# The constants of a kernel's own list schedule: delay, occupancy, a shared port and the delay of a transfer

## The chip, the cores and the metric

The kernel runs on one core of one Trainium2 chip. The metric is the device time of one execution in microseconds (us), as the median of several runs. The engines are TensorE (PE, with its weight loads as PEld), VectorE (DVE), ScalarE (ACT), GpSimd (POOL) and SyncE (SP), which issues all the transfers of this kernel.

## The reference

The reference is a two-layer diffusion trunk over 1024 latent tokens and 256 context tokens, all of width 1024, in fp32. Cut to what matters:

```python
for l in range(DEPTH):                                   # DEPTH = 2
    sh1, sc1, g1, sh2, sc2, g2 = ada_params(c[:, None, :], ada_w[l], ada_b[l])
    h  = modulate(rms_norm(x,  norm1_g[l]), sh1, sc1)    # latent, 1024 tokens
    hc = modulate(rms_norm(cx, norm1_g[l]), csh1, csc1)  # context, 256 tokens
    p = h @ w_in[l]                                      # 1024 -> 2304 columns
    y_a = fourier_mix(p[..., 0:256])                     # 2-D FFT as matmuls
    y_b = neighbourhood_attention(q, k, v, k_ctx, v_ctx, na_rpb[l], rows)
    y_c = spatial_gating(...)                            # gelu, layer norm, 128x128 mixing
    o_d = diff_latent(...)                               # softmax(s1) - lam * softmax(s2), then @ v
    y = concatenate([y_a, y_b, y_c, diff_post(o_d)]) @ w_out[l]
    # layer 0 does the same for the context tokens
    x = x + g1 * y
    h2 = modulate(rms_norm(x, norm2_g[l]), sh2, sc2)
    x = x + g2 * sq_relu_mlp(h2, w_ff1[l], w_ff2[l])     # 1024 -> 4096 -> 1024
return rms_norm(x, final_g)
```

## The kernel before

Tokens lie in three blocks: two of 512 latent tokens (0 and 1) and one of 256 context tokens (2). Activations are held with channels on the partitions. Every fp32 product is made of three products of a shorter type, FP32R: an operand is split into a high and a low part (`hh`/`hl` for activations, `wh`/`wl` for weights), and `mm3` adds high by high, high by low and low by high into one bank of PSUM. The high part is a copy on ScalarE. The low part is a subtraction on GpSimd or VectorE. Weights that layer 1 needs, and part of those of layer 0's MLP, are split ahead of time and kept in DRAM as `wd`; they are loaded as `wh`/`wl` by plain transfers.

The stages follow one another in time, with some overlap: the start (root mean squares `nacc`, `nss`, `nr`, `nrb`; the modulation parameters `ada`, whose weighted sums `aa` run on VectorE and GpSimd; the first projections `pj`, `pv`), the mixers of layer 0, its MLP, the mixers of layer 1, its MLP (the products `sx`, `sy`), and the final norm. In an attention mixer, scores (`ds`, or `nsl` and `nsc`) come from TensorE. VectorE takes their maximum and ScalarE the exponential `e`. VectorE and GpSimd normalise `e`, TensorE transposes it (`tp`), ScalarE and VectorE evacuate the transpose as a high and a low part (`pt`, `npt`), and TensorE multiplies these by the values (`pvd`, `pvn`).

No instruction is issued where it is written. The program text records every operation in a `Plan`, with the operations on which it depends and a rank. `Plan.cost` gives each a time, and `Plan.flush` makes a list schedule over the five engines: it takes the engine that can start earliest, and on it, among the operations that are ready by the plan's own clock, the one of lowest rank. An operation counts as ready once all that it waits for has ended by that clock, plus `LAT` where the two are on different engines. All instructions are then emitted in this one order (all of them at L286), and each engine of the chip works its own instructions off in that order, waiting where a result is not there yet. So the plan's clock sets the order alone; it delays nothing by itself. In the plan, an instruction of SP takes 0.06 us to issue, a transfer holds the transfer clock for its bytes at 320 bytes per ns (at least 0.3 us), and its result is there a fixed time later.

Of the kernel before, what the change touches and what calls it, by code (L numbers as in the profile page):

```python
# [11 lines left out]
F32R = mybir.dt.float32r  # L12
# [4 lines left out]
PSUM = bass.MemoryType.PSUM  # L17
# [16 lines left out]
class Plan:  # L34
# [3 lines left out]

    LAT = 0.13

    def __init__(self, tc):
        self.tc, self.nc = tc, tc.nc
        self.rank = self.erank = 0.0
        self.ops = []
        self.done = 0
        self.hist = {}
        self.tiles = {}
        self.tags = {}  # L50
        self.masks = {}
        self.free = {}
        self.idle = []
        self.dma_free = 0.0


    def pool(self, pool):
# [102 lines left out]
    def cost(self, eng, method, outs, ins, kw):  # L160
        def width(a):
            n = 1
            for _, k in a.ap[1:]:
                n *= k
            return n

        n = max(width(a) for a in outs + ins)
        if eng == "tensor":
            n = width(outs[0])
            c = 1 if ins[0].dtype == F32R else 2 if method == "transpose" else 4  # L170
            return max(n, 128 if c == 4 else 64) * c / 2400.0
        if eng == "sync":
            b = 4
            for _, k in outs[0].ap:
                b *= k
            return b
        if eng == "scalar":
            return 0.093 + n / 1200.0 + (0.13 if kw.get("accum_out") is not None else 0.0)
        if eng == "vector":
            ptr = any(isinstance(kw.get(k), bass.AP) for k in ("scalar", "scalar1", "scalar2"))  # L180
            fast = method in ("tensor_scalar", "tensor_copy", "memset") and all(a.space != PSUM for a in outs + ins)
            return 0.065 + 0.065 * ptr + n / (1920.0 if fast else 960.0)
        return 0.1 + n / 470.0


    def flush(self):
        ops, base = self.ops, self.done
        n = len(ops)
        left, succ, ready = {}, {}, {}
        tiles, tags = self.tiles, self.tags  # L190
        waiting = {}
        engines = ("tensor", "vector", "scalar", "gpsimd", "sync")
        future = {e: [] for e in engines}
        avail = {e: [] for e in engines}

        def allocate(key):
            q = tags[key]
            while q[2] < q[0] and q[1]:
                t = q[1].pop(0)
                q[2] += 1  # L200
                tiles[t][2] = q[3]
                for i in waiting.pop(t, ()):
                    settle(i, q[3])

        def settle(i, t):
            ready[i] = max(ready[i], t)
            left[i] -= 1
            if left[i] == 0:
                heapq.heappush(future[ops[i][0]], (ready[i], i))

        pend = {}
        for i in range(base, n):
            for t in ops[i][5]:
                pend[t] = pend.get(t, 0) + 1

        def release(t):
            q = tags[tiles[t][0]]
            if q[1]:
                q[2] -= 1
                q[3] = max(q[3], tiles[t][3])  # L220
                allocate(tiles[t][0])
            else:
                self.idle.append(t)

        idle, self.idle = self.idle, []
        for t in idle:
            if t not in pend:
                release(t)
        for key in tags:
            allocate(key)  # L230
        for i in range(base, n):
            o = ops[i]
            left[i] = 1
            ready[i] = 0.0
            for j in o[4]:
                if j >= base:
                    left[i] += 1
                    succ.setdefault(j, []).append(i)
                else:
                    ready[i] = max(ready[i], ops[j][8])  # L240
            for t in o[5]:
                if tiles[t][2] is None:
                    left[i] += 1
                    waiting.setdefault(t, []).append(i)
                else:
                    ready[i] = max(ready[i], tiles[t][2])
            settle(i, 0.0)
        order = []
        while len(order) < n - base:
            best = None  # L250
            for e in engines:
                f = self.free.get(e, 0.0)
                if avail[e]:
                    s = f
                elif future[e]:
                    s = max(f, future[e][0][0])
                else:
                    continue
                if best is None or s < best[0]:
                    best = (s, e)  # L260
            s, e = best
            while future[e] and future[e][0][0] <= s:
                _, i = heapq.heappop(future[e])
                heapq.heappush(avail[e], (ops[i][6], i))
            _, i = heapq.heappop(avail[e])
            o = ops[i]
            if e == "sync":
                self.free[e] = s + 0.06
                self.dma_free = max(self.dma_free, s) + max(0.3, o[7] / 320e3)
                end = self.dma_free + 1.9  # L270
            else:
                end = s + o[7]
                self.free[e] = end
            o[8] = end + self.LAT
            order.append(i)
            for k in succ.get(i, ()):
                settle(k, end if e == "tensor" and ops[k][0] == "tensor" else o[8])
            for t in o[5]:
                pend[t] -= 1
                tl = tiles[t]  # L280
                tl[3] = max(tl[3], o[8])
                if pend[t] == 0:
                    release(t)
        for i in order:
            o = ops[i]
            ins = o[1](*o[2], **o[3])  # L286
            self.tc.keep_in_program_order(ins)
            o[1] = o[2] = o[3] = None
        self.done = n
# [1861 lines left out]
```

## Time and profile before

| what | value |
|---|---|
| time, median of 3 runs (lowest to highest) | 3067.94 us (3063.21 to 3068.87) |
| the profiled execution: its time, its span | 3058.95 us, 3057.1 us |
| mean granted TensorE clock of the profiled execution | 0.972 |
| busy share of the span: PE, DVE, ACT, POOL | 93%, 66%, 45%, 24% |
| moved from and to HBM | 388.58 MB, 162.88 MB |

The profile is of one execution on the chip. Times in it are us from the start of the span. "Idle before" is the time for which an engine had nothing to do before an instruction, and the name behind it is what released that instruction. The granted clock is a share of TensorE's full 2.4 GHz; at the lower of its two levels, 1.2 GHz, the same product takes twice as long.

### The profile page before, as it was taken

How to read it: one execution, taken by the hardware profiler on the slowest of the kernel's cores; microseconds unless marked ns; L12 is line 12 of the kernel's file. 1: busy time of each engine (PE TensorE's matmuls, PEld its weight loads, DVE VectorE, ACT ScalarE, POOL GpSimd, SP SyncE). 2: the span in 40 equal slices, each digit the busy share in tenths (PEclk: the TensorE clock that was granted, in tenths of full speed). 3: DMA queues.
4: the chain of work that ended last, by engine and by line, in shares of the span. 5: the costliest groups of instructions: out<-in, count | busy, mean ns of one | idle time of the engine just before them, and what ended most of it. 6: DMA issues, size and time to landing. Idle time of an engine off the chain costs nothing. (4 is left out here: it accounts for less than half of the span.)

```text
span 3057.1 us, 42917 instructions
## 1 busy us (share of the span) xinstructions
PE 2854.0 (93%) x14994; PEld 2348.7 (77%) x14994; DVE 2028.2 (66%) x3721; ACT 1370.7 (45%) x2974; POOL 738.7 (24%) x507
## 2 busy tenths in 40 slices
PE   6798999999999999999999888998998999999997
PEld 3776787776788888888888777877786778878876
DVE  7577886695766676664433737786784875576765
ACT  5476565584423233222122426555573544454332
POOL 5235222343521121121111303311110022122200
PEclk8998999999999999999999999999999999999998
DMA  6644345777347886673111463455688664464465
GB/s 229 194 133 134 106 125 153 245 251 251 98 146 260 274 275 217 221 239 126 59 46 38 145 200 126 132 163 160 215 298 290 226 215 144 145 217 150 150 230 176
DMA packets 291632, 550.60 MB, mean 180 GB/s; under 512 B 35924, under 2 KB 84692, under 8 KB 288344
## 3 DMA queue, kind: packets, MB, share of 16 engines
q1 hardware_dynamic: 291416, 547.86, 54.6%
q8 instruction: 118, 1.93, 0.3%
q14 instruction: 98, 0.80, 0.1%
HBM read 388.58 MB, written 162.88 MB: 180 GB/s over the span
## 5 line engine op out<-in xcount | busy, mean ns | idle before, releaser
L286 POOL TENSOR_TENSOR wl<-wr,wh 128x512 fp32r<-128x512 f32 (+2 forms) x260 | 361.1, 1410 | 928.8 <-ACT wh L286 887.9
L286 PE MATMUL sx<-bq,sh 128*128 128x512 f32 x2304 | 548.5, 396 | 9.5 <-ACT q L286 3.4
L286 PEld LDWEIGHTS sx<-bq,sh 128*128 128x128 f32 x2304 | 430.5, 188 | 121.1 <-DVE bq L286 6.5
L286 DVE TENSOR_REDUCE mx<-ds 128x1 f32<-128x512 f32 (+1 forms) x320 | 218.5, 686 | 135.0 <-PE ds L286 133.1
L286 ACT ACTIVATE e<-ds,nm 128x512 f32<-128x512 f32 (+1 forms) x400 | 241.3, 611 | 122.8 <-DVE nm L286 112.9
L286 ACT ACTIVATE wh<-wr 128x512 fp32r<-128x512 f32 (+2 forms) x260 | 152.4, 614 | 315.5 <-issue 137.3
L286 PE MATMUL f<-hidh,wh 128*128 128x512 f32 (+1 forms) x768 | 276.8, 360 | 6.3 <-ACT hh L286 4.1
L286 PE MATMUL f<-hidl,wh 128*128 128x512 f32 (+1 forms) x768 | 275.8, 359 | 0.0
L286 PE MATMUL f<-hidh,wl 128*128 128x512 f32 (+1 forms) x768 | 275.6, 359 | 0.0
L286 PE MATMUL f<-hh,wh 128*128 128x512 f32 (+1 forms) x768 | 274.5, 357 | 0.0
L286 PE MATMUL f<-hl,wh 128*128 128x512 f32 (+1 forms) x768 | 274.2, 357 | 0.0
L286 PE MATMUL f<-hh,wl 128*128 128x512 f32 (+1 forms) x768 | 274.2, 357 | 0.0
L286 PE MATMUL pj<-hh,wh 128*128 128x512 f32 (+1 forms) x512 | 194.5, 380 | 24.0 <-DMA wh<-wd 11.5
L286 DVE SCALAR_TENSOR_TENSOR x<-f,ada,x 128x512 f32<-128x512 f32 (+1 forms) x192 | 125.6, 659 | 135.3 <-PE f L286 134.7
L286 PE MATMUL pj<-hl,wh 128*128 128x512 f32 (+1 forms) x512 | 193.9, 379 | 2.0 <-POOL hl L286 1.2
L286 PE MATMUL pj<-hh,wl 128*128 128x512 f32 (+1 forms) x512 | 192.7, 377 | 1.0 <-DMA wl<-wd 1.0
L286 ACT ACTIVATE sh<-wq 128x512 fp32r<-128x512 f32 x160 | 99.3, 628 | 203.4 <-DMA wd<-sh 47.9
L286 POOL TENSOR_TENSOR e<-e 128x1280 f32<-128x1280 f32 (+1 forms) x36 | 98.4, 2733 | 380.4 <-DVE e L286 226.1
L286 POOL TENSOR_TENSOR ws<-wq 128x512 f32<-128x512 f32 x54 | 77.7, 1439 | 421.5 <-DVE sh L286 205.6
L286 PE MATMUL ds<-dks,dqs 128*128 128x512 f32 (+1 forms) x400 | 144.1, 397 | 31.0 <-ACT e L286 17.7
L286 DVE TENSOR_TENSOR fr<-fr 128x512 f32<-128x512 f32 (+1 forms) x96 | 83.6, 870 | 132.7 <-ACT fr L286 132.4
L286 PEld LDWEIGHTS f<-hidh,wh 128*128 128x128 f32 x768 | 145.4, 189 | 30.4 <-ACT hh L286 4.5
(316 smaller groups left out, 6555.8 us busy)
## 6 DMA issues: line engine op xcount, KB each, us to landing
wd<-sh SPq DMA_DIRECT2D x99, 512.0 KB, 4.0
wr<-in_w_ff SPq DMA_DIRECT2D x144, 256.0 KB, 3.1
ar<-in_ada_w SPq DMA_DIRECT2D x112, 256.0 KB, 4.0
bq<-hid SPq DMA_DIRECT2D x24, 1024.0 KB, 6.5
wq<-in_w_ff1s SPq DMA_DIRECT2D x76, 256.0 KB, 2.9
sh<-wd SPq DMA_DIRECT2D x66, 256.0 KB, 4.4
wq<-in_w_ff2s SPq DMA_DIRECT2D x64, 256.0 KB, 3.8
wr<-in_ada_w SPq DMA_DIRECT2D x48, 256.0 KB, 3.9
```

The source lines that it names most:

```text
L286: ins = o[1](*o[2], **o[3])
```

## The change

The change edits the numbers and rules of `Plan` alone; what is computed and the set of instructions stay as they are.

- `LAT`, the delay between an operation's end and its use on another engine, is 0.22 us instead of 0.13.
- The occupancy of an FP32R product is max(0.112, 0.006 + n/2265) instead of max(n, 64)/2400 (for n = 512: 0.232 instead of 0.213; for 256: 0.119 instead of 0.107). Transposes and fp32 products stay within a few ns.
- On ScalarE the fixed part is 0.055 if an input lies in PSUM and 0.105 if not (0.093 before), and an accumulated sum adds 0.17 instead of 0.13. On GpSimd the time is 0.13 + n/457 instead of 0.1 + n/470 (for n = 512: 1.25 instead of 1.19). On VectorE a scalar operand from memory adds 0.06 instead of 0.065.
- A new rule, `shares`, names the operations that use a port common to VectorE and GpSimd: every operation of GpSimd, and those of VectorE that read nothing from PSUM and have two inputs or are a `tensor_scalar` or `tensor_copy`. In `flush` such an operation starts no earlier than the last one that shared the port has ended.
- The delay of a transfer after its bytes is 2.6 us instead of 1.9.

```diff
-    LAT = 0.13
+    LAT = 0.22
...
+        self.port = 0.0
...
             n = width(outs[0])
-            c = 1 if ins[0].dtype == F32R else 2 if method == "transpose" else 4
-            return max(n, 128 if c == 4 else 64) * c / 2400.0
+            if ins[0].dtype == F32R:
+                return max(0.112, 0.006 + n / 2265.0)
+            if method == "transpose":
+                return 0.107
+            return max(0.224, n / 600.0)
...
         if eng == "scalar":
-            return 0.093 + n / 1200.0 + (0.13 if kw.get("accum_out") is not None else 0.0)
+            near = any(a.space == PSUM for a in ins)
+            return (0.055 if near else 0.105) + n / 1200.0 + (0.17 if kw.get("accum_out") is not None else 0.0)
...
-            return 0.065 + 0.065 * ptr + n / (1920.0 if fast else 960.0)
-        return 0.1 + n / 470.0
+            return 0.065 + 0.06 * ptr + n / (1920.0 if fast else 960.0)
+        return 0.13 + n / 457.0
+
+    def shares(self, o):
+
+        if o[0] == "gpsimd":
+            return True
+        if o[0] != "vector":
+            return False
+        ins = [v for k, v in o[3].items() if k in ("in_", "in0", "in1") and isinstance(v, bass.AP)]
+        if any(a.space == PSUM for a in ins):
+            return False
+        return len(ins) > 1 or o[9] in ("tensor_scalar", "tensor_copy")
...
                 self.dma_free = max(self.dma_free, s) + max(0.3, o[7] / 320e3)
-                end = self.dma_free + 1.9
+                end = self.dma_free + 2.6
             else:
+                if self.shares(o):
+                    s = max(s, self.port)
+                    self.port = s + o[7]
                 end = s + o[7]
```

What this does to the order is seen in the instructions of each engine. The order of the two MLPs is nearly the same before and after; within the mixers most instructions move by a few places. Three places follow. In a row stand the line, the operation, the output and the inputs with their buffer numbers, and the shape; xN is N such in a row.

The first place is the start. On GpSimd, once the last `aa` is done, before:

```order
L286 TENSOR_TENSOR aa_124<-aa_124,adaw_116 128x512 x7
L286 TENSOR_TENSOR hl0_134<-x0_93,hh0_133 128x512
L286 TENSOR_TENSOR hl0_134<-x0_95,hh0_133 128x512
L286 TENSOR_TENSOR hl0_134<-x0_94,hh0_133 128x512
L286 TENSOR_TENSOR hl0_134<-x0_93,hh0_133 128x512
L286 TENSOR_TENSOR wvl_206<-wr_203,wvh_205 128x512
```

And on GpSimd after:

```order
L305 TENSOR_TENSOR aa_124<-aa_124,adaw_116 128x512 x7
L305 TENSOR_TENSOR wvl_206<-wr_203,wvh_205 128x512
L305 TENSOR_TENSOR wvl_206<-wr_204,wvh_205 128x512
L305 TENSOR_TENSOR wvl_210<-wr_207,wvh_209 128x512
L305 TENSOR_TENSOR wvl_210<-wr_208,wvh_209 128x512
L305 TENSOR_TENSOR hl0_134<-x0_93,hh0_133 128x512
L305 TENSOR_TENSOR hl0_134<-x0_94,hh0_133 128x512
```

The four low parts of the value weights (`wvl`) move ahead of the four low parts of block 0's activations (`hl0`), which the first projections read. On TensorE, the sums of squares of block 1 (`nss_143`) stand here before, behind 32 of the 48 products of the first two projections (`pj_185`, `pj_196`):

```order
L286 MATMUL pj_185<-hl0_134,wh_183 128x512
L286 MATMUL pj_185<-hh0_133,wl_184 128x512
L286 MATMUL pj_196<-hl0_134,wh_194 128x512
L286 MATMUL nss_143<-ones_79,nacc_135 128x1 x4
L286 MATMUL pj_196<-hh0_133,wl_195 128x512
L286 MATMUL pj_196<-hh0_133,wh_194 128x512
```

And after, the same sums stand here:

```order
L305 MATMUL ada_132<-ones_79,aa_124 128x1 x4
L305 MATMUL pj_185<-hh0_133,wh_183 128x512
L305 MATMUL pj_196<-hh0_133,wh_194 128x512
L305 MATMUL nss_143<-ones_79,nacc_135 128x1 x4
L305 MATMUL pj_185<-hl0_134,wh_183 128x512
L305 MATMUL pj_185<-hh0_133,wl_184 128x512
```

They move up to behind the first two of the 48 products.

The second place is in the differential attention of layer 1, on TensorE, where scores (`ds`) alternate with the gating mixer's `sgo` and a projection (`pj_3320`). Before:

```order
L286 MATMUL sgo_3317<-fs_3270 64x128
L286 MATMUL ds_3640<-dks_3550,dqs_3622 128x256
L286 MATMUL ds_3640<-dks_3551,dqs_3622 128x256
L286 MATMUL sgo_3317<-fs_3270 64x128 x3
L286 MATMUL ds_3642<-dks_3551,dqs_3622 128x512
L286 MATMUL pj_3320<-hh0_2975,wh_3318 128x512
L286 MATMUL pj_3320<-hl0_2976,wh_3318 128x512
```

And after, the last `sgo` and what follows them:

```order
L305 MATMUL ds_3640<-dks_3550,dqs_3622 128x256
L305 MATMUL ds_3640<-dks_3551,dqs_3622 128x256
L305 MATMUL sgo_3317<-fs_3270 64x128 x2
L305 MATMUL pj_3320<-hh0_2975,wh_3318 128x512
L305 MATMUL pj_3320<-hl0_2976,wh_3318 128x512
L305 MATMUL pj_3320<-hh0_2975,wl_3319 128x512
```

A little further on, after:

```order
L305 MATMUL pj_3320<-hh0_2975,wh_3318 128x512
L305 MATMUL pj_3320<-hl0_2976,wh_3318 128x512
L305 MATMUL ds_3642<-dks_3551,dqs_3622 128x512
L305 MATMUL pj_3320<-hh0_2975,wl_3319 128x512
L305 MATMUL pj_3320<-hh0_2975,wh_3318 128x512
L305 MATMUL pj_3320<-hl0_2976,wh_3318 128x512
L305 MATMUL ds_3643<-dks_3551,dqs_3622 128x512
```

Eleven products of `pj_3320` now stand ahead of `ds_3642`, where none stood before (some of them lie between the two pieces above).

The third place is in the neighbourhood attention of layer 1, on TensorE, beside the output projection `wo`. Before:

```order
L286 MATMUL tp_4246<-ident_78,e_4236 128x128 x4
L286 MATMUL wo_4320<-fs_4303,wh_4317 128x512
L286 MATMUL wo_4320<-yl4_4304,wh_4317 128x512
L286 MATMUL wo_4320<-fs_4303,wl_4318 128x512
L286 MATMUL wo_4324<-fs_4301,wh_4321 128x512
L286 MATMUL tp_4247<-ident_78,e_4236 128x128 x2
L286 MATMUL wo_4324<-fs_4302,wh_4321 128x512
L286 MATMUL pvn_4248<-npt_4243,nsb_4141 128x256
```

And after:

```order
L305 MATMUL tp_4246<-ident_78,e_4236 128x128 x4
L305 MATMUL tp_4247<-ident_78,e_4236 128x128 x2
L305 MATMUL pvn_4248<-npt_4243,nsb_4141 128x256
L305 MATMUL pvn_4248<-npt_4244,nsb_4141 128x256
L305 MATMUL wo_4339<-yh1_4325,wh_4340 128x512
```

The transposes `tp_4245`, `tp_4246` and `tp_4247` are evacuated into slices of `npt_4243` (high) and `npt_4244` (low), which the products `pvn_4248` read. The `wo` products that stood between the transposes and these products have moved to other places.

## Rows read from the trace of the kernel before

**Rows 1.** The page's first part: busy time of each engine, its share of the span, and its instructions.

```profile
PE 2854.0 (93%) x14994; PEld 2348.7 (77%) x14994; DVE 2028.2 (66%) x3721; ACT 1370.7 (45%) x2974; POOL 738.7 (24%) x507
```

**Rows 2.** Busy time of each engine (with its instructions), the granted TensorE clock, the share of the DMA engines and GB/s, in six stretches: start, mixers of layer 0, its MLP, mixers of layer 1, its MLP, final norm.

```profile
0.00:150.00 150.00, 103.97 (x527) 80.14 (x528) 92.36 (x169) 71.57 (x131) 56.06 (x44) 0.90 0.64 211
150.00:930.00 780.00, 727.94 (x4195) 588.89 (x4194) 569.88 (x1230) 429.36 (x1086) 269.99 (x194) 0.97 0.52 167
930.00:1720.00 790.00, 788.79 (x4089) 667.80 (x4088) 442.84 (x627) 212.95 (x386) 165.44 (x116) 1.00 0.52 172
1720.00:2475.00 755.00, 673.39 (x3793) 563.75 (x3792) 544.48 (x1168) 403.06 (x989) 140.59 (x77) 0.95 0.62 200
2475.00:2960.00 485.00, 484.27 (x2074) 387.97 (x2073) 318.00 (x430) 227.31 (x347) 99.22 (x70) 1.00 0.50 171
2960.00:3057.00 97.00, 75.62 (x326) 60.14 (x324) 60.68 (x102) 26.47 (x38) 7.43 (x6) 0.90 0.59 201
```

**Rows 3.** The waits of TensorE over the whole span: what waited for what, us in total, how often, the longest.

```profile
PE nss L286 <- DVE nacc L286: 23.6, 7, 14.9
PE ds L286 <- ACT e L286: 17.7, 24, 2.5
PE pj L286 <- DMA wh<-wd: 11.5, 2, 8.2
PE nrb L286 <- DVE nr L286: 11.4, 5, 4.3
...
PE drb L286 <- DVE drw L286: 6.0, 3, 3.0
...
PE fmid L286 <- DVE m L286: 4.8, 1, 4.8
PE tp L286 <- DVE e L286: 4.8, 6, 1.5
...
PE tp L286 <- DVE npt L286: 3.0, 5, 1.3
```

**Rows 4.** The timeline of TensorE at the start: start in us, us, engine, line, operation, out<-in, how many, and in brackets the idle time before it with its releaser.

```profile
65.28 0.40 PE L286 MATMUL pj<-hl,wh 128*128 128x512 f32 x1
69.47 1.05 PE L286 MATMUL nss<-ones,nacc 128*128 128x1 f32 x8 [3.80 <-DVE nacc L286]
...
71.10 0.63 PE L286 MATMUL pj<-hl,wh 128*128 128x512 f32 x1
71.53 0.63 PE L286 MATMUL pj<-hh,wl 128*128 128x512 f32 x1
...
94.90 0.77 PE L286 MATMUL pj<-hh,wh 128*128 128x512 f32 x1 [6.16 <-DVE nr L286]
```

**Rows 5.** The timelines of VectorE and GpSimd at the start, columns as in rows 4.

```profile
19.61 0.75 DVE L286 SCALAR_TENSOR_TENSOR aa<-adaw,sc,aa 128x512 f32<-128x512 f32 x1
...
36.65 8.34 DVE L286 SCALAR_TENSOR_TENSOR aa<-adaw,sc,aa 128x512 f32<-128x512 f32 x5
...
53.87 1.28 POOL L286 TENSOR_TENSOR hl<-x,hh 128x512 fp32r<-128x512 f32 x1 [6.41 <-ACT x L286]
...
62.29 6.58 POOL L286 TENSOR_TENSOR wvl<-wr,wvh 128x512 fp32r<-128x512 f32 x4 [1.14 <-ACT wvh L286]
```

**Rows 6.** The timelines of TensorE and ScalarE at the second place, columns as in rows 4.

```profile
1989.02 0.65 PE L286 MATMUL sgo<-fs 128*64 128x128 f32 x6
1991.95 0.50 PE L286 MATMUL ds<-dks,dqs 128*128 128x512 f32 x1 [2.28 <-ACT e L286]
...
1992.57 0.63 PE L286 MATMUL pj<-hl,wh 128*128 128x512 f32 x1
1993.00 0.63 PE L286 MATMUL pj<-hh,wl 128*128 128x512 f32 x1
...
1991.12 0.69 ACT L286 ACTIVATE e<-ds,nm 128x512 f32<-128x512 f32 x1
```

**Rows 7.** The timelines of TensorE, ScalarE and VectorE at the third place, columns as in rows 4.

```profile
2310.60 0.62 PE L286 MATMUL tp<-ident,e 128*128 128x128 f32 x4
...
2311.30 0.39 PE L286 MATMUL wo<-yl,wh 128*128 128x512 f32 x1
2311.53 0.40 PE L286 MATMUL wo<-fs,wl 128*128 128x512 f32 x1
...
2312.44 0.52 PE L286 MATMUL pvn<-npt,nsb 128*128 128x256 f32 x3
...
2311.37 0.60 ACT L286 ACTIVATE npt<-tp 128x512 fp32r<-128x512 f32 x1
...
2312.14 0.75 DVE L286 SCALAR_TENSOR_TENSOR xo<-wo,ada,xo 128x512 f32<-128x512 f32 x1
2312.81 0.68 DVE L286 TENSOR_TENSOR npt<-tp,npt 128x512 fp32r<-128x512 f32 x1
```

**Rows 8.** The transfers: a stretch of SP's queue, TensorE behind it (columns as in rows 4), and from the page's part on issues two groups with the KB of each and the median us from issue to landing.

```profile
2084.18 7.58 SPq L286 DMA_DIRECT2D nvw<-vt  x16
...
2097.96 0.79 PE L286 MATMUL pj<-hh,wh 128*128 128x512 f32 x1 [8.21 <-DMA wh<-wd]
...
wr<-in_w_ff SPq DMA_DIRECT2D x144, 256.0 KB, 3.1
...
sh<-wd SPq DMA_DIRECT2D x66, 256.0 KB, 4.4
```

## What the change was predicted to do

> **What bounds the kernel now.** I read the page's busy times first: TensorE is busy for 2854.0 us of a span of 3057.1, far ahead of VectorE with 2028.2 [rows 1]. So about 203 us of the span are left on TensorE, and a change of order can only win there. The table by stretch says where they lie [rows 2]: 46 us at the start (150 less 103.97), 52 in the mixers of layer 0, 1 in its MLP, 82 in the mixers of layer 1, 1 in its MLP, 21 in the final norm. The two MLPs keep TensorE busy at a granted clock of 1.00. Their order is all but unchanged, so I expect 0 from these 1275 us. What is at stake are the start and the mixers. The granted clock is 0.90, 0.97 and 0.95 there, so a gap costs a little more than its length.
>
> The waits name the causes [rows 3]. TensorE waits for the sums of squares (`nss`, 23.6, of which 14.9 once, at the very start, for the first data), for exponentials before it may write the next scores (`ds` behind `e`, 17.7 in 24 pieces), for loads of weights (`pj`, 11.5), for `nrb` 11.4, `drb` 6.0, `fmid` 4.8, and for transposes and their evacuation (`tp` 4.8 and 3.0). These are many short waits for chains on other engines. TensorE had work elsewhere in its queue, but the plan took the chain for shorter than it is and put the waiting instruction too early.
>
> **The change part by part.** It removes and adds no instruction. Each term is a sum of waits gone and waits come. To find the places I went through the two orders and added up TensorE's work between each waiting instruction and the one that starts its chain (0.23 us for a product of 512 columns, from 2311.30 to 2311.53 in [rows 7]). That work is the cover.
>
> *A, the start.* Before, `nss` waits 3.80 us behind 32 of the 48 first products, and later a product waits 6.16 [rows 4], since block 1's modulation comes late. After the first wait the products run 0.43 apart (71.10 to 71.53) instead of 0.23, the lower of the two clocks; for some eight products that is 1.6. Afterwards, block 1's sums stand 30 products further ahead and its chain begins earlier. I let both waits go, with the 1.6 and some 2 of small ones behind them: -13.6. Against it, GpSimd now makes four `wvl` before the first `hl0`. They took 6.58 [rows 5]. TensorE's third product reads that `hl0`, and all 46 left stand behind it: +6.6 if nothing hides it. The third product starts later, but from there on the products need not stop. The sum is -7, with the ends -13.6 (the `wvl` are hidden) and +6.6 (the whole `wvl`, no wait saved).
>
> *B, waits that get more cover.* The second place is the clearest. `ds` waits 2.28 for `e` [rows 6]; eleven products now lie ahead of it, 11 x 0.233 = 2.6, so the wait goes. What follows it at the lower clock (0.43 from 1992.57 to 1993.00) runs faster too. There are 33 places of this kind in the mixers. What they can give is limited by the waits of their kinds: `ds` 17.7, `nss` beyond the start 4.9 (23.6 - 14.9 - 3.8), `nrb` some 3 (11.4 less two long ones of about 4.2 at the start and the end), `drb` 6.0, `fmid` 4.8, `tp` 7.8, in all 44 [rows 3]. At some of them the order is as before, two of the three `drb` for example. I take somewhat over half, -25. The ends are -40 (nearly all) and -12 (a quarter).
>
> *C, waits that get less cover.* At 31 places less work than before lies between transposes and the products that read them. At the third place [rows 7] the four transposes end at about 2311.0, ScalarE's `npt` starts at 2311.37, and VectorE's runs from 2312.81 to 2313.49, some 2.4 us after the transposes; 0.75 of this is `xo`, which stands ahead of it on VectorE. After the change there are two transposes, one `wo` and a few `pvn` of about 0.12 in between, some 1.2. So 0.45 (without `xo`) to 1.2 is missing there. Behind the waiting `pvn` stands all of TensorE's queue. Over 31 places nothing is the lower end (the plan now counts the longer delay, so it moved them where its clock shows the evacuation as done), and 1.3 at each, 40, the upper. I take 0.55, near the lower value of this place, as half of the places lose less cover than this one: +17. I believe B more than C, because B's waits are measured and C's rest on queues that move as well.
>
> *D, the transfers.* Landing takes 3.1 to 4.4 us for 256 KB [rows 8]. The plan's old figure for this is 0.82 + 1.9 + 0.13 = 2.85, the new one 3.64, so by the rows the new one is nearer. It can only help loads that are issued in time. The longest wait for one, 8.21 us at 2097.96, comes from SP, which is busy with sixteen `nvw` stores for 7.58 us ahead of the load, 0.47 each; the plan counts 0.06 for each, before and after, and the place is the same in SP's queue. I take -2, with ends 0 and -6. Here a rule of the Trainium skill speaks against the edit: "DMA: Bandwidth & Descriptors", section "Anatomy of one DMA", puts a transfer's time at about 2.0 us plus its bytes at 436 GB/s, for another kind of issue than this kernel's. For 256 KB that is an estimate of 2.6 us, nearer to the old figure than to the new one; D would be 0 and the time 3051. The rows show longer times than this rule for every group here.
>
> *E, the clock.* Each gap of over 2 us is followed by products at 0.43 instead of 0.23 [rows 4, 6], about 1.4 us for seven. Three such gaps go in B, one or two may come in C: -2, with ends -4 and +2.
>
> The occupancies of ScalarE, GpSimd and VectorE and the port have no term of their own; they show in A to C through the order. The port's part is real: five `aa` took 8.34 on VectorE while GpSimd worked on its own, 1.67 each, one without that 0.75 [rows 5]. But the engines exclude each other before as after, and only the plan's knowledge of it is new.
>
> The sum: -7 - 25 + 17 - 2 - 2 = -19. The profiled execution took 3058.95 us, 9 less than the median of 3067.94 and less than the fastest of its three runs. I take the difference off the median: 3067.94 - 19 = **3049 us**.
>
> **The rivals.** A difference of 0.2%, 6.1 us, is about what a measurement of this kernel can tell from no change.
>
> 1. *The gain without its price.* C is 0 and B is 40: -7 - 40 - 2 - 3 = -52, 3016; with part of it 3014 to 3030. For it speaks that the new durations match the rows (0.232 against 0.23 apart for a product). Against it, 31 places with less cover are many for none to wait.
> 2. *The waits only move.* B and C cancel, and the start gives nothing: 3062 to 3074. For it: by counts of cover alone the two are nearly even, 33 places against 31, and VectorE, 66% busy, is a second queue in which every saved wait may meet another operation.
> 3. *Slower: the transposes.* C is the full 40 and B only 12: -7 - 12 + 40 - 3 = +18, 3086, and with the upper end of A 3100. The mechanism is the third place, 31 times over: `pvn` stands directly behind its transposes, while `npt` waits on VectorE behind work of other stages. With B at 12 it decides from C = 28 on (0.9 us a place), with B at 25 from 41 on.
> 4. *Slower at the start.* GpSimd's `wvl` hold it and the port for 6.58 us ahead of `hl0`, no wait of the start goes, and the mixers come out even: +6.6, less 0 to 4 of D and E, 3070 to 3076. The Trainium skill, "SBUF — State Buffer", section "Who interferes with whom", calls the port pair an exclusive lock which whoever comes first holds for the whole instruction; by that rule VectorE's own `hl0` would be held up beside the four `wvl` as well. The 1.67 against 0.75 above agrees.
>
> **How the numbers follow.** My forecast, 3030 to 3061, has 0.42; rival 1 0.15, rival 2 0.19, rival 3 0.14, rival 4 0.10 (0.04 of it within 0.2%). Faster is 0.42 + 0.15 = 0.57, the same 0.19 + 0.04 = 0.23, slower 0.14 + 0.06 = 0.20. The range for 8 in 10 is 3020 to 3080: it leaves out half of rival 1 (0.07) and most of rival 3 (0.13). The likeliest case's own range is 3030 to 3061.
>
> **What would show it.** For A: no wait of `nss` behind products at 65 us, in its place one of `pj` for `hl` of up to 6.6, and the wait of 6.16 gone. For B: `ds` behind `e` at 12 or less in total instead of 17.7, and no wait at the second place. For C: the waits of `tp`, `pvn` and `pvd` for `e`, `npt` and `pt` up by some 17 in sum. For D: the wait of 8.2 is still there. In the table by stretch, TensorE's idle time should fall from 46 to about 40 at the start and by some 12 in all over both mixers, with both MLPs at 1. I am wrong if the waits for `npt`, `pt` and `e` grow by over 35 us, if a transfer that was on time comes late behind SP's queue, or if idle time moves into the MLPs or the final norm, to which I gave nothing.

## The result and the profile after

The changed kernel took 3025.64 us (3020.74 to 3026.14) against 3067.78 us of the kernel before in the same comparison: a ratio of 0.9862, with a 95% interval of 0.9845 to 0.9879. That is 42 us less where 19 were forecast. The time lies in the stated range of 3020 to 3080, but the gain is over twice the forecast.

The profiled execution took 3025.96 us with a span of 3024.2, so here the trace agrees with the median. The trace of before was 9 us under its median. Between the two traces, 33 us are to be explained, and 9 of the 42 lie between that trace and the runs.

The page's first part of the changed kernel, columns as in [rows 1]:

```profile
PE 2854.4 (94%) x14994; PEld 2357.3 (78%) x14994; DVE 2005.3 (66%) x3721; ACT 1363.8 (45%) x2974; POOL 728.5 (24%) x507
```

TensorE is busy for the same 2854 us. VectorE and GpSimd are busy for 23 and 10 us less with the same instructions, so they hold each other up less here. That is no sign of the port's rule: kernels below that have it lie between 2005 and 2031 on VectorE, and those without it between 2011 and 2039.

The busy times of the changed kernel by stretch, columns as in [rows 2]; the borders are moved with the stages, which now come up to 33 us earlier:

```profile
0.00:150.00 150.00, 107.63 (x538) 82.96 (x539) 96.52 (x178) 72.96 (x137) 57.60 (x45) 0.86 0.65 215
150.00:911.00 761.00, 726.39 (x4178) 587.70 (x4177) 548.12 (x1218) 425.54 (x1080) 259.79 (x193) 0.97 0.54 170
911.00:1702.00 791.00, 790.56 (x4096) 670.71 (x4095) 436.89 (x625) 210.32 (x383) 161.17 (x118) 1.00 0.51 173
1702.00:2442.00 740.00, 669.20 (x3791) 564.73 (x3790) 541.99 (x1171) 400.79 (x989) 138.38 (x77) 0.95 0.62 201
2442.00:2927.00 485.00, 483.78 (x2072) 389.70 (x2071) 320.68 (x431) 227.72 (x348) 104.10 (x70) 1.00 0.49 172
2927.00:3024.20 97.20, 76.85 (x329) 61.55 (x327) 61.14 (x103) 26.48 (x38) 7.42 (x6) 0.88 0.60 204
```

TensorE's idle time at the start goes from 46 to 42 us, in the mixers of layer 0 from 52 to 35, in those of layer 1 from 82 to 71. Both MLPs and the final norm stay within about 1 us. So the mixers give 28 us, where the forecast had 12.

TensorE's waits in the changed kernel, columns as in [rows 3]:

```profile
PE nss L305 <- DVE nacc L305: 15.5, 3, 14.7
PE ds L305 <- ACT e L305: 12.7, 22, 2.3
...
PE nrb L305 <- DVE nr L305: 7.2, 2, 4.3
PE pj L305 <- DMA wh<-wd: 6.9, 2, 5.4
...
PE pv L305 <- DVE dl L305: 5.8, 2, 3.8
PE drb L305 <- DVE drw L305: 5.5, 3, 3.0
...
PE pj L305 <- POOL hl L305: 4.8, 1, 4.8
...
PE pvd L305 <- DVE pt L305: 3.1, 5, 1.5
...
PE tp L305 <- DVE e L305: 2.4, 3, 1.8
...
PE tp L305 <- DVE npt L305: 1.7, 4, 0.5
```

Against [rows 3], the sums of squares fall from 23.6 to 15.5, of which 14.7 is the unchanged wait for the first data. `nrb` falls from 11.4 to 7.2, `ds` behind `e` from 17.7 to 12.7, and `tp` behind `e` and `npt` on VectorE from 7.8 to 4.1. Some rows are new, the largest of them `pv` behind `dl` (5.8); `pj` behind GpSimd's `hl` grows from 1.2 to 4.8 at the start. All waits together fell from 189.4 to 156.0 us. By kind: `nss` and `nrb` -12, all waits for transfers -12 (42.2 to 29.8), scores -6, transposes and the products behind them -2 (13.6 to 11.4), the rest 0.

### The profile page after: what moved, and what is told of

Its sections match the earlier page's. It is cut to its first block, busy times and chain, and to the rows that moved or that the text cites. A ratio compares the mean times of both kernels' runs of the same rounds, so it can differ in the third digit from the quotient of the medians.

```text
span 3024.2 us, 42917 instructions
## 1 busy us (share of the span) xinstructions
PE 2854.4 (94%) x14994; PEld 2357.3 (78%) x14994; DVE 2005.3 (66%) x3721; ACT 1363.8 (45%) x2974; POOL 728.5 (24%) x507
## 5 line engine op out<-in xcount | busy, mean ns | idle before, releaser
L305 POOL TENSOR_TENSOR wl<-wr,wh 128x512 fp32r<-128x512 f32 (+2 forms) x260 | 350.4, 1368 | 923.8 <-ACT wh L305 877.8
L305 PE MATMUL pj<-hh,wh 128*128 128x512 f32 (+1 forms) x512 | 196.4, 384 | 26.1 <-DMA wh<-wd 6.9
L305 PEld LDWEIGHTS f<-hh,wh 128*128 128x128 f32 x768 | 145.0, 189 | 28.4 <-ACT fr L305 2.8
```

## The three places

The start, the timelines of TensorE and GpSimd in the changed kernel, columns as in [rows 4]:

```profile
55.49 1.86 PE L305 MATMUL nss<-ones,nacc 128*128 128x1 f32 x8 [0.39 <-DVE nacc L305]
62.20 0.79 PE L305 MATMUL pj<-hl,wh 128*128 128x512 f32 x1 [4.84 <-POOL hl L305]
...
67.31 0.80 PE L305 MATMUL pj<-hl,wh 128*128 128x512 f32 x1 [2.18 <-DVE hl L305]
...
97.38 0.76 PE L305 MATMUL pj<-hh,wh 128*128 128x512 f32 x1 [5.10 <-DVE nr L305]
...
55.13 5.79 POOL L305 TENSOR_TENSOR wvl<-wr,wvh 128x512 fp32r<-128x512 f32 x4 [4.01 <-ACT wvh L305]
60.86 3.96 POOL L305 TENSOR_TENSOR hl<-x,hh 128x512 fp32r<-128x512 f32 x3
```

The wait of `nss` behind the products went (3.80 to 0.39), and in its place the third product waits 4.84 for `hl0`, which GpSimd begins at 60.86, when the four `wvl` are done. The later wait of 6.16 [rows 4] went down to 5.10 only.

The second place, the timeline of TensorE:

```profile
1975.52 0.39 PE L305 MATMUL pj<-hl,wh 128*128 128x512 f32 x1
1976.13 0.50 PE L305 MATMUL ds<-dks,dqs 128*128 128x512 f32 x1 [0.22 <-ACT e L305]
```

`ds` waits 0.22 where it waited 2.28 [rows 6], with eleven products of `pj` ahead of it.

The third place, the timelines of TensorE and VectorE:

```profile
2289.58 0.62 PE L305 MATMUL tp<-ident,e 128*128 128x128 f32 x4
2290.70 0.44 PE L305 MATMUL tp<-ident,e 128*128 128x128 f32 x2 [0.49 <-DVE npt L305]
2291.14 0.51 PE L305 MATMUL pvn<-npt,nsb 128*128 128x256 f32 x2
...
2291.12 0.69 DVE L305 TENSOR_TENSOR npt<-tp,npt 128x512 fp32r<-128x512 f32 x1
```

TensorE waits 0.49 here. That this is near the lower value that the prediction gave for this place (0.45) is chance, for it is another wait. The products `pvn` do not wait; the next two transposes do, until VectorE has emptied a bank of PSUM with an earlier `npt`. The low part of these four transposes is ready at 2291.81 (2291.12 + 0.69), 1.6 us after they end in the rows, where it was 2.3 before [rows 7]: `xo` no longer stands ahead of it on VectorE.

## Experiments

Every kernel below has the same instructions and differs in the plan's numbers and rules alone. The theories: **the delay** (longer delays lay more work over each chain), **the port** (the plan's clock for VectorE and GpSimd ran ahead of the chip's), and, as a rival to both, **scatter** (a greedy list schedule jumps with any edit). A ratio is to the kernel before on the same chip, with its 95% interval.

### One part alone

By its code, the plan adds the delay wherever one operation reads another's result, unless both are on TensorE, and not only between two engines. So a longer delay also lengthens a chain of steps on VectorE alone.

lat_only:

```diff
-    LAT = 0.13
+    LAT = 0.22
```

> The kernel before with the delay alone changed, 0.13 to 0.22. Theory of the delay (the plan took the chains over other engines for shorter than they are, and the longer delay lays more work over each): most of the 42 us comes from here, -25 to -35 us against the kernel before. Theory of the port (the plan's clock of VectorE and GpSimd ran ahead of the chip's, and knowing this makes their chains shorter): -10 us or less. Theory of scatter (a greedy list schedule jumps with any edit of its numbers, by some 10 us either way): anything from -15 to +15.

occ_only has the new numbers of `cost` and nothing else:

```diff
+            if ins[0].dtype == F32R:
+                return max(0.112, 0.006 + n / 2265.0)
...
+        return 0.13 + n / 457.0
```

> The kernel before with the occupancies of TensorE, ScalarE, VectorE and GpSimd alone changed. Theory of the delay: -5 us, since TensorE's 0.232 instead of 0.213 lays slightly less, not more, work over a chain in the plan. Theory of the port: -5. Theory of scatter: -15 to +15.

port_only has `shares` and the lines for it in `flush`:

```diff
+                if self.shares(o):
+                    s = max(s, self.port)
+                    self.port = s + o[7]
```

> The kernel before with the shared port alone added. Theory of the port: -15 to -25 us, the waits of transposes and of the products behind their evacuation fall, and VectorE's busy time falls from 2028 by some 15. Theory of the delay: 0 to -8. Theory of scatter: -15 to +15.

dma_only:

```diff
-                end = self.dma_free + 1.9
+                end = self.dma_free + 2.6
```

> The kernel before with the transfer's delay alone changed, 1.9 to 2.6. Theories of the delay and of the port: -2 us (0 to -6), since the longest wait for a load is SP's issue and stays. Theory of scatter: -15 to +15.

| part alone | us | ratio (interval) |
|---|---|---|
| lat_only | 3075.34 | 1.0043 (1.0028 to 1.0058) |
| occ_only | 3145.44 | 1.0259 (1.0237 to 1.0281) |
| port_only | 3072.01 | 1.0022 (1.0013 to 1.0031) |
| dma_only | 3103.01 | 1.0121 (1.0106 to 1.0136) |

No part alone is faster. As accounts of the whole gain, the theory of the delay and that of the port both fall here: neither part gives 15 us or more, and all four lose. The occupancies and the transfer's delay lose more than even the scatter that I had allowed. The signs expected of the port did not come either: VectorE's busy time, which was to fall by some 15, is 2030.5 in port_only (2028.2 before), and the waits of transposes rose.

### The change without one part

no_port leaves out the three lines of `flush` above, no_occ puts back the numbers of `cost`, no_lat puts back 0.13, no_dma 1.9. One of the diffs, against the changed kernel:

```diff
-    LAT = 0.22
+    LAT = 0.13
```

> The changed kernel without the shared port; delay, occupancies and transfer as changed. Each of the four parts alone came out slower than before (by 6 to 80 us). Theory of the set (the parts belong together: the plan's clock must be right for all engines, a part alone makes it wrong elsewhere): losing one part loses part of the 42 us, and the kernel lies between, 3030 to 3060. Theory of scatter (each set of numbers gives an order that is some 30 us better or worse by chance, and the kernels before and after are both lucky ones): anything between 3030 and 3130, with no relation to the part.

> The changed kernel with the occupancies of before. Theory of the set: 3030 to 3060; since TensorE's 0.213 instead of 0.232 makes the plan see less cover than there is, the loss is small. Theory of scatter: 3030 to 3130.

> The changed kernel with the delay of before, 0.13. Theory of the set: a loss of most of the gain, 3045 to 3065, because this part sets the cover of every chain. Theory of scatter: 3030 to 3130.

> The changed kernel with the transfer's delay of before, 1.9. Theory of the set: 3025 to 3035, as few waits hang on it. Theory of scatter: 3030 to 3130.

| the change without | us | ratio (interval) |
|---|---|---|
| the port | 3081.6 | 1.0062 (1.0047 to 1.0077) |
| the occupancies | 3125.59 | 1.0197 (1.0178 to 1.0216) |
| the delay | 3080.94 | 1.0054 (1.0039 to 1.0069) |
| the transfer's delay | 3051.53 | 0.9958 (0.9944 to 0.9972) |

All four are slower than the changed kernel, and the parts do not add: three of the four are slower than the kernel before as well, where the theory of the set had 3030 to 3065. The occupancies, which I had thought the smallest part, cost most when they are missing and when they stand alone. This fits a set that belongs together, but a lucky order in the kernels before and after would look the same. So the next runs made edits that say nothing of the chip.

### Neighbours of both kernels

Against the changed kernel (after_...) and against the kernel before (before_...), one number each, for example:

```diff
-    LAT = 0.22
+    LAT = 0.21
```

> The changed kernel with a delay of 0.21 instead of 0.22: an edit that tells the plan nothing better or worse of the chip. Theory of the set (the plan gains because its numbers fit the chip): 3018 to 3036, since 0.01 us is far below what any wait here measures. Theory of scatter (the order of a greedy list schedule jumps with any edit, and 0.22 is a lucky draw): 3040 to 3090.

> The changed kernel with a delay of 0.23 instead of 0.22. Theory of the set: 3018 to 3036. Theory of scatter: 3040 to 3090, and not the same value as with 0.21.

> The kernel before with a delay of 0.12 instead of 0.13. Theory of the set: 3060 to 3072, or a little slower. Theory of scatter: 3075 to 3120, as 0.13 is a lucky draw too.

> The kernel before with a delay of 0.14 instead of 0.13. Theory of the set: 3058 to 3068. Theory of scatter: 3075 to 3120.

> The changed kernel with a transfer's delay of 2.5 instead of 2.6. Neighbours of the changed kernel with a delay of 0.21 and 0.23 took 3045 and 3042, the kernel itself 3026. If the set of numbers sets a level of about 3035 to 3045 with a scatter of some 10 around it: 3025 to 3055. If the level is that of all other kernels here, 3065 to 3105, and the three were lucky: 3060 or more.

> The changed kernel with a transfer's delay of 2.7 instead of 2.6. Level of the set: 3025 to 3055. Lucky draws: 3060 or more.

> The kernel before with a delay of 0.11 instead of 0.13. Its neighbours with 0.12 and 0.14 took 3107 and 3067. If the numbers of before set a level of their own, about 3080, with scatter: 3065 to 3110, and none of its neighbours comes under the neighbours of the changed kernel. If there are no levels, only scatter: 3040 to 3110.

> The kernel before with a delay of 0.15 instead of 0.13. Level of its own with scatter: 3065 to 3110. Scatter alone: 3040 to 3110.

| neighbour of the changed kernel | us | ratio | neighbour of the kernel before | us | ratio |
|---|---|---|---|---|---|
| delay 0.21 | 3045.0 | 0.9952 | delay 0.11 | 3090.57 | 1.0079 |
| delay 0.23 | 3041.76 | 0.9925 | delay 0.12 | 3106.67 | 1.0139 |
| transfer 2.5 | 3052.38 | 0.9957 | delay 0.14 | 3067.47 | 1.0017 |
| transfer 2.7 | 3040.12 | 0.9913 | delay 0.15 | 3067.59 | 1.0010 |

The intervals are within 0.0025 of the ratios. By these, an edit of 0.01 us in the delay moves the time by 0.63 to 0.90% (19 to 28 us) on the one side and by 0.17 to 1.39% (5 to 43 us) on the other. So scatter is real. But there are two levels as well: the four neighbours of the changed kernel have a mean ratio of 0.9937, those of the kernel before 1.0061. All of the first lie below 1, and none of the second does. The distance of the levels is 1.24%, 38 us. Both kernels of this case lie below the mean of their neighbours, the one before by 0.6% (19 us), the changed one by 0.75% (23 us). So the gain of 42 us is about the distance of the levels, and the luck of the two orders nearly cancels. Four neighbours on each side give these means only roughly: by their own spread, the distance is uncertain by an estimated 10 us.

The neighbours also change what the first two tables say. Alone, the delay (1.0043), the port (1.0022) and the transfer's delay (1.0121) lie no further off than the neighbours of the kernel before (1.0010 to 1.0139), so these runs do not show that any of the three does harm alone. The change without the transfer's delay (0.9958) is not apart from the neighbours of the changed kernel (0.9913 to 0.9957), so that this part is needed is not shown. Clear of the neighbours are the occupancies alone, and the change without the port, the occupancies or the delay. Each of these is one order without neighbours of its own.

### What the parts do to the waits

The traces of these runs tell more than their times. One kind of wait follows one part in all twenty kernels, and another does in most. The first are the sums of squares. In the kernel with the port alone, and then in the changed kernel without it (the last column is the longest wait, here the first data):

```profile
PE nss L302 <- DVE nacc L302: 15.3, 2, 14.8
...
PE nrb L302 <- DVE nr L302: 5.8, 3, 4.3
```

```profile
PE nss L302 <- DVE nacc L302: 23.7, 8, 14.8
...
PE nrb L302 <- DVE nr L302: 20.5, 5, 12.1
```

Over all kernels: `nss` behind `nacc` is 14.8 to 16.2 in the eleven with the port, and 22.0 to 26.5 in the nine without. With the port, `nrb` behind `nr` is 5.8 to 8.5 (14.0 without the new occupancies), without it 11.4 to 26.0. The seven additions of `nacc` for a block run on VectorE with both inputs in SBUF, while GpSimd splits weights. One such place in the kernel before, on VectorE, GpSimd and TensorE:

```profile
1707.24 1.59 DVE L286 TENSOR_TENSOR nacc<-nacc,nsq 128x512 f32<-128x512 f32 x1 [0.76 <-ACT nsq L286]
...
1705.74 2.54 POOL L286 TENSOR_TENSOR wl<-wr,wh 128x512 fp32r<-128x512 f32 x2 [2.59 <-ACT wh L286]
...
1708.88 0.83 PE L286 MATMUL nss<-ones,nacc 128*128 128x1 f32 x6 [1.14 <-DVE nacc L286]
```

The last addition takes 1.59 us beside GpSimd's `wl`, where one took 0.69 just before (at 1705.12), and `nss` waits 1.14 for it. A plan that lets both run at once calls for `nss` too early. This is the port's own gain on waits, some 8 us on `nss` and some 3 or more on `nrb`. In port_only it is given back elsewhere: transposes and the products behind them wait 27.2 there, 13.6 before.

The second are the scores that wait for keys which go through DRAM (`dks`). In the kernel before, from the same view as [rows 3]:

```profile
PE ds L286 <- DMA dks<-dk: 9.7, 3, 5.5
```

With a transfer's delay of 1.9 or 2.1 this sum is 2.8 to 11.2 in ten kernels, 7.2 in the mean. With 2.5 to 2.7 it is 0 to 3.9 in ten others, 1.1 in the mean, and the changed kernel has no such row. The ranges overlap, and other parts lower this sum too: it is 2.8 in lat_only and 3.1 in no_dma, both with 1.9. The pairs that differ in the 1.9 or 2.1 and the 2.6 alone give -8.4 (the kernel before and dma_only), -3.1 (no_dma and the changed kernel) and -2.2 (the two kernels with issue45 below). So this part gains an estimated 2 to 8 us on these waits, and dma_only loses it elsewhere: its `ds` wait 30.5 for `e`. The landing itself, from the list of transfers of the kernel before, columns as in [rows 8]:

```profile
dks<-dk SPq DMA_DIRECT2D x32, 320.0 KB, 5.0
```

The other waits follow no part so plainly. Transposes and the products behind them wait most in no_occ, 39.1 in all, of which the largest rows are:

```profile
PE pvn L301 <- DVE ny L301: 8.2, 8, 2.5
...
PE tp L301 <- DVE npt L301: 7.8, 14, 1.2
...
PE tp L301 <- POOL e L301: 5.9, 4, 2.9
```

With both the port and the new occupancies they are 10.6 to 28.8, with the port and the old ones 27.2 and 39.1. These ranges overlap, and without the port the old occupancies give 9.9 to 26.4. That the occupancies and the port belong together is suggested by this, not shown.

Waits are not all that differs. The first line of the page of occ_only:

```profile
PE 2910.2 (93%) x14994; PEld 2365.4 (75%) x14994; DVE 2023.2 (64%) x3721; ACT 1367.8 (44%) x2974; POOL 734.3 (23%) x507
```

Its span is 3143.0, 86 us more than before. Of these, 56 are TensorE's busy time (2910.2 against 2854.0 for the same instructions) and only 30 are idle time; the mean granted clock is 0.963 against 0.972. In no_occ, 35 of 99 us over the changed kernel are busy time (2889.5 against 2854.4), at 0.961 against 0.970. Between the two sets of neighbours, 14 of the 40 us of the mean spans are busy time. So a part of what an order costs shows in no wait at all. That it comes from more products at the lower level of the clock fits the granted clocks, but how much of it does was not measured.

### SP's issue time

The wait of 8.21 behind the `nvw` stores [rows 8] is 5.38 in the changed kernel. From its trace, SP's queue and TensorE:

```profile
2052.91 16.11 SPq L305 DMA_DIRECT2D nvw<-vt  x32
...
2075.13 0.79 PE L305 MATMUL pj<-hh,wh 128*128 128x512 f32 x1 [5.38 <-DMA wh<-wd]
```

The plan still has 0.06 us for an issue, and 32 took 16.11, 0.50 each. Two kernels give the plan 0.45:

```diff
-                self.free[e] = s + 0.06
+                self.free[e] = s + 0.45
```

> The changed kernel with SP's issue time of 0.45 us in the plan instead of 0.06. If the plan gains by numbers that fit the chip, the wait of some 5 us behind the nvw stores shrinks to 2 or less, the waits of TensorE for loads fall from 29.8 to 15 to 20 in sum, and the time is 3010 to 3035. If the scatter is larger than this gain: 3035 to 3060, with the waits for loads lower all the same. If SP's issue is no bound of anything but that one place, and the plan now starts loads too late: 3060 and more.

> As the run before, with a transfer's delay of 2.1 instead of 2.6, in case the 2.6 stood in for the issue time that the plan lacked. If it did: as fast as the run before or faster, 3005 to 3035. If 2.6 is the landing time as such: slower than the run before by 5 to 15.

Measured: 3038.14 (ratio 0.9918, 0.9900 to 0.9936) and, with 2.1, 3047.1 (0.9946, 0.9929 to 0.9963). Neither beats the changed kernel; the first lies among its neighbours. The waits for transfers did not fall as expected, 36.1 against 29.8. SP's queue and TensorE in issue45:

```profile
2078.98 7.45 SPq L305 DMA_DIRECT2D nvw<-vt  x16
2086.53 0.37 SPq L305 DMA_DIRECT2D wl<-wd  x1
...
2092.49 0.79 PE L305 MATMUL pj<-hh,wh 128*128 128x512 f32 x1 [6.68 <-DMA wh<-wd]
```

A plan that knows the price still puts the sixteen stores ahead of the loads. By its code it takes the operation of lowest rank among those that are ready, and a right clock does not change the ranks; that this is the cause was not tried. Nothing shows that the 2.6 stood in for the issue time: with 2.1 the waits of `dks` rise from 3.9 to 6.1. The 9 us between the two kernels lie within the scatter.

## Why the prediction was wrong

Its mechanism, short waits of TensorE in the mixers for chains that the plan took for too short, was right, and so were the places where nothing happens (both MLPs, the final norm). The size of the gain was off, by these steps.

- **C, waits that get less cover (+17), is the term that failed.** All waits of `tp`, `pvn` and `pvd` went from 13.6 to 11.4, a gain of 2. The products themselves, `pvd` and `pvn`, wait 5.8 us in the whole changed kernel and 5.6 before. Even if all of the 5.8 stood at the 31 places, it would be 0.19 at each, where 0.55 was forecast. The mistake was to measure the new cover against the chain's old length. Counted over the two traces, there are 40 chains whose cover falls by over 0.5 us, to less than 2.5. In these the low part of the evacuation ends 1.8 us after its transposes, 2.2 before (means). Over all 264 evacuations it stays at 2.1. So the chains are not shorter in general: products came nearer where the chain had become shorter, as the queues on VectorE and GpSimd moved too. The prediction had named this as a reason for the lower end (the plan moves them where its clock shows the evacuation as done) and then not taken it.
- **D, the transfers (-2, ends 0 and -6), was too small.** TensorE's waits for transfers fell by 12.4. The largest single part is `dks`, 9.7 before and none after, a row that I did not use; by the pairs above, 2 to 8 us of it come from the 2.6. That the wait behind the `nvw` stores would stay was right (8.2 to 5.4). The Trainium skill's rule ("DMA: Bandwidth & Descriptors", "Anatomy of one DMA"), 2.0 us plus the bytes at 436 GB/s for transfers that GpSimd issues, makes an estimate of 2.75 us for the 320 KB of `dks`. The trace does not agree for these transfers of SyncE: 5.0 is the median, and the waits of `dks` fall in each pair with the longer delay. For whole times the scatter is too large to tell by this. That every group here is longer than the rule, as the prediction says, holds for the loads of 256 KB (2.9 to 4.4 before), but not for some stores (`hid` from `t` and from `bb`, `dv`: 2.3 to 2.5).
- **B, more cover (-25).** At the 33 places the idle time fell from 16.6 to 1.9, by 14.7; this is my own count over the two traces, which no row here shows. By the rows of the kinds (`ds` behind `e`, `nss` beyond the first data and the start, `nrb`, `drb`, `fmid`) it fell from 44.8 to 26.1, by 19. Both are in the stated range of 12 to 40 and below the 25. The limit of 44 by kinds had counted waits at other places too. `ds` came to 12.7 (12 or less was named).
- **A, the start (-7).** Idle time fell by 4. The wait for `hl0` came as described (4.84, at most 6.6), and another of 2.18 came. The wait of 6.16 that was to go is still 5.10, since the prediction had its cause wrong: it is not block 1's modulation. ScalarE and VectorE before, then in the changed kernel:

```profile
79.70 1.52 ACT L286 ACTIVATE hh<-x,ada,A 128x512 fp32r<-128x512 f32 x2 [1.93 <-DVE x L286]
...
94.35 0.41 DVE L286 TENSOR_TENSOR vt<-pv,vt 128x256 fp32r<-128x256 f32 x1
```

```profile
78.75 1.52 ACT L305 ACTIVATE hh<-x,ada,A 128x512 fp32r<-128x512 f32 x2
...
94.67 0.63 ACT L305 ACTIVATE dh<-draw 128x512 fp32r<-128x512 f32 x1 [4.88 <-DVE draw L305]
...
96.81 0.42 DVE L305 TENSOR_TENSOR vt<-pv,vt 128x256 fp32r<-128x256 f32 x1 [0.19 <-ACT vt L305]
```

Block 1's first `hh`, which the waiting product reads, is ready by 81.2 before and 80.3 after. But the product writes a bank of PSUM that a `pv` had filled, and it starts 0.14 to 0.15 us after the second `vt` has emptied that bank (94.76 and 97.23). The profile names `nr`, the instruction next to that `vt` on VectorE. ScalarE's part of this evacuation stands behind `dh`, which waited 4.88 for `draw` (3.23 before). An earlier chain of block 1 does not by itself end this wait. Nor did that chain come much earlier:

```profile
71.43 0.16 DVE L305 SCALAR_TENSOR_TENSOR nr<-rs_u,nr 128x4 f32<-128x4 f32 x1
...
74.59 1.06 PE L305 MATMUL nrb<-ident,nr 128*128 128x128 f32 x8
```

The sums stand 14 us earlier, but the eleven steps of the inverse root behind them took 13 us, from 58.47 on, instead of 6 (70.56 to 76.53). They ran partly beside GpSimd's `wvl` and among other work of VectorE, and `nrb` is only 3 us earlier (77.80 before).

- **E, the clock (-2).** The granted clock is 0.86, 0.97 and 0.95 in the start and the mixers, 0.90, 0.97 and 0.95 before [rows 2]. No gain shows.
- **The sum.** With C and D as measured (-2 and -12) and B and A too (-15 and -4), it is -33, which is the difference of the two traces. That these four agree so closely is partly chance, as the kinds overlap at the start, and with B by its rows (-19) the sum is -37.
- **The offset.** Taking the difference off the median assumed that the trace lies under the median by the same 9 us after. It did not, which gave the other 9 us. That trace was of an execution with a high granted clock: beside the runs above, executions of the kernel before at 0.972 took 3056 to 3060 us, and those at 0.965 took 3071.
- **The rivals.** Rival 1, the gain without its price, came nearest (C at nothing; its 3014 to 3030 holds the time), with a chance of 0.15. Its C was right, but the time is luck in part: it had B at 40 and little from D, where 15 to 19 and 12 were measured, and it too was taken off the median. Rival 3's mechanism did not appear, and rival 4's came with 4.84 and was paid for by other waits of the start.

No step of the prediction had the scatter. As it went by the two orders themselves and not by the plan's numbers, the scatter is not what made it wrong. But differences of 5 to 43 us from an edit of 0.01 us mean that the 42 us are the gain of this one order, and tell of the numbers only by the two levels.

What stays open: why the occupancies cost 80 us alone and 100 when they are left out, of which the waits hold 30 and 64; and how far the two levels would hold with more neighbours.

## What to carry to other kernels

When an order moves, count each wait against the chain as the new order leaves it, with the queues of the other engines, and not against the length that it had. Before a gain from a planner's numbers is put down to one of them, run neighbours that say nothing of the chip: here they moved the time by 5 to 43 us, and only the means of several told the level from the luck. That a planner's numbers belong together is suggested here and not shown: all four parts together reach the lower level, but alone only the occupancies are clear of the neighbours, and slower. And before a wait is put down to the engine that the profile names, see whether what the instruction reads was long there: here it was a bank of PSUM that was missing.

## What the runs showed of the hardware

VectorE's smallest instructions are held up beside GpSimd as long as large ones. From the timelines of VectorE and GpSimd in the changed kernel, the same instruction alone and beside GpSimd:

```profile
21.28 0.15 DVE L305 TENSOR_TENSOR rs_u<-rs_u,rs_a 128x4 f32<-128x4 f32 x1
...
25.68 1.22 DVE L305 TENSOR_TENSOR rs_u<-rs_u,rs_a 128x4 f32<-128x4 f32 x1
...
18.77 1.26 POOL L305 TENSOR_TENSOR aa<-aa,adaw 128x512 f32<-128x512 f32 x1
21.46 8.57 POOL L305 TENSOR_TENSOR aa<-aa,adaw 128x512 f32<-128x512 f32 x5 [1.44 <-issue]
```

Four columns take 0.15 us alone, while GpSimd is idle, and 1.22 while GpSimd adds its `aa`, about the length of one GpSimd instruction (1.26). By these two figures, each step that meets one costs 1.07 us more, so a chain of eleven such small steps, as in the inverse root, can lose several us (an estimate).
